# A hybrid decoder layer on one core: softmax statistics exchanged by ScalarE and GpSimd, opening weights ranked first on VectorE, last weight sums formed in the fourth product

## The chip, the cores and the metric

The kernel runs as one program on one NeuronCore of a Trainium2 chip. The metric is the device time of that core in microseconds (us); lower is better. The engines are named PE (TensorE, matrix products), PEld (its weight loads), DVE (VectorE), ACT (ScalarE), POOL (GpSimd) and SP (SyncE, which here only issues transfers).

## The reference

One layer over 1024 tokens of width 1024, float32 throughout:

```python
def reference(x, w_in, ..., w_out, ln1_w, ln1_b, mlp_w1, mlp_w2, ln2_w, ln2_b):
    h = hybrid_mixer(x, ...)     # z = x @ w_in (1024 -> 2816 columns), split into
                                 #  (A) state-space groups, (B) 4 retention heads,
                                 #  (C) 8 dilated-attention heads; y @ w_out
    x = layer_norm(ALPHA * x + h, ln1_w, ln1_b)
    h = square(relu(x @ mlp_w1)) @ mlp_w2      # 1024 -> 4096 -> 1024
    return layer_norm(ALPHA * x + h, ln2_w, ln2_b)

def dilated_attention_mixer(q, k, v):          # branches (128, 1), (512, 4), (2048, 16)
    outs, lses = branch results and their log-sum-exps
    return sum(softmax(lses)[..., i] * outs[i] for i in range(3))
```

## The kernel before, in words

**Precision.** Every large product is made of three float32r products: each operand is cast to float32r by ACT (the high part), the rest is subtracted by DVE or POOL (the low part), and `mm3` (from L402) issues high x high, high x low, low x high.

**Who sets the order.** The program is a set of coroutines with ranks. A planner with its own clock starts, at each step, the coroutine step that can begin earliest; where starts tie, the lower rank goes first. What comes out is a fixed order of instructions for every engine, executed in that order; semaphores only hold an instruction until its data are there. Tiles of 128x1024 ("units") come from one pool of 32, and a load has to wait for a free unit. Each kind of use leaves a number of units spare.

**Attention.** Heads go in pairs. `far` makes the scores of one head for the later half of the tokens in two layouts (`y` = 0 and 1), with row minima and exponential sums in a small tile `stat`. `join(p)` then has to bring the two layouts' statistics together: they live on other partitions of each other, so 16 blocks of 32 partitions are copied crosswise. From both statistics it works out one factor for each row, `fac`, by which `high` scales the far scores before it transposes them and multiplies them with the values. Meanwhile PE has the matmuls of the input projection (`dense`) and of the output projection to fill its time.

**First LayerNorm.** `out_a` finishes the output projection tile by tile; `add_a`, `norm1` and `x_operands` normalise each of the 8 token tiles on DVE, ACT and POOL, store it, transpose it on PE and split it into the operands of the first MLP product. Those for products 1 and 2 (tile `XOB`) need token tiles 0 to 3 only; products 6 and 5 (`XOA`), 7, 4 and 3 need all eight.

**The MLP products.** Both are done by a seven-product scheme on 2x2 blocks (products numbered 1 to 7, in the order `UORD = (1, 6, 5, 7, 2, 4, 3)` for the first). The first one runs over 16 quads of 256 hidden columns. Of the first `NF = 4` quads ("opening quads") products 1 and 2 are done early, in `mlp`, because they need only `XOB`: `up_load` brings half of such a quad's weights, `up_cast` casts them and `up_lo` makes the low parts (tile `wop`). Then come products 6, 5, 7, 4, 3 of each opening quad. Product 7 adds to the bank of product 6, product 4 adds to it again, and between them DVE must read the bank out (`up_evac`, tiles `u` and `rb`).

**The second MLP product** goes product by product (`DORD = (1, 5, 6, 3, 2, 7, 4)`), each over 8 parts `j` of the hidden width, 24 matmuls for each part. `down_load` brings for each part one tile of stored activations (`rraw`) and one or two of weights (`wraw`); `down_split` forms the weight sum where one is needed, in place in a resident tile `K`, and splits both into `doh` and `dol`. Loads run ahead by two parts, in the last two products by four.

**Second LayerNorm.** As soon as products 7 and 2 are in, tiles 0 to 3 are normalised under the last product; tiles 4 to 7 follow at the end. `layer_norm` multiplies by the weights on DVE and adds the bias on DVE below the column `LNB[t]` and else on POOL.

Of the kernel before, what the change touches and what calls it, by code (L numbers as in the profile page):

```python
# [16 lines left out]
ALU = mybir.AluOpType  # L17
# [10 lines left out]
NQ = FF // 256  # L28
NF = 4
# [7 lines left out]
LNF = "AAAADDD"  # L37
LNN = (1024,) * 5 + (512, 512)
LNW = (0,) * 6 + (512,)
LNB = (0,) * 7  # L40
TIE = 0.02
LAG = 2
DEPTH = 5
# [254 lines left out]
async def when(w, early=0.0):  # L298
    if isinstance(w, str):
        await ask(("flag", w))  # L300
    elif w:
        await ask(("data", w, early))
# [3 lines left out]
def trunk_kernel(ctx: ExitStack, tc: tile.TileContext, t_in, out):  # L306
    nc = tc.nc
    clock = Clock()
    pe, act, dve, pool, sp = (Engine(e, n, clock) for e, n in (
        (nc.tensor, "pe"), (nc.scalar, "act"), (nc.vector, "dve"), (nc.gpsimd, "pool"), (nc.sync, "sp")))  # L310
# [25 lines left out]
    st_ = Stream(clock)  # L336
# [13 lines left out]
    def free(*tiles):  # L350

        for t in tiles:
            if isinstance(t, (list, tuple)):
                free(*t)
            else:
                room = st_.room[tags.pop(t.tensor.name)]
                room[0] += 1
                room[1].append(clock.last[t.tensor.name])

    def U(shape, dt=F32, name="u", spare=2):  # L360
        return take(up, shape, dt, "u", NU, name, spare)
# [7 lines left out]
    def PM(shape=(128, 512), name="pm"):  # L369
        return take(pp, shape, F32, "main", 3, name, 0)  # L370

    def PS(shape=(128, 512), name="ps"):
        return take(pp, shape, F32, "side", 5, name, 0)

    def SM(shape, name, bufs=2):
        return take(sm, shape, F32, name, bufs, name, 0)

    def f(ap):
        return ap.bitcast(F32)

    async def tt(eng, o, a, b, op):
        await eng.tensor_tensor(out=o, in0=a, in1=b, op=op)
# [7 lines left out]
    M, A_, SUB = ALU.mult, ALU.add, ALU.subtract  # L390
# [796 lines left out]
    def counted(key, n):  # L1187
        count[key] = count.get(key, 0) + 1
        return count[key] == n
# [61 lines left out]
    async def far(i_, h):  # L1251
# [39 lines left out]
        if counted(("far", p), 2):  # L1291
            st_.add(1.7, join(p))

    async def join(p):

        stat = T["stat", p]
        for i in range(4):
            for j in range(4):
                a, b = slice(32 * i, 32 * i + 32), slice(32 * j, 32 * j + 32)
                await act.copy(stat[b, 2, i], stat[a, 1, j])  # L1300
                await dve.tensor_copy(stat[b, 3, i], stat[a, 0, j])
        await when([stat])
        both = stat.rearrange("p (o y) j e k -> p o (y j e) k", o=2)
        wk = await SM([128, 3, 16], "wk")
        tmp = await SM([128, 2, 16], "wk2")
        await tt(dve, wk[:, 0], both[:, 0, :, 0], both[:, 1, :, 0], ALU.min)
        await tt(dve, tmp, wk[:, 0:1].to_broadcast([128, 2, 16]), both[:, :, :, 0], SUB)
        await act.activation(tmp, tmp, AF.Exp)
        await tt(dve, wk[:, 1:3], tmp, both[:, :, :, 1], M)
        await tt(dve, wk[:, 1], wk[:, 1], wk[:, 2], A_)  # L1310
        await dve.reciprocal(wk[:, 2], wk[:, 1])
        fac = await SM([128, 2, 4, 2], "fac")
        await tt(dve, fac.rearrange("p y j e -> p (y j e)"), tmp[:, 0], wk[:, 2], M)
        free(wk, tmp, stat)
        T["fac", p] = fac
        flag(f"fac{p}")
# [192 lines left out]
    async def layer_norm(t, w, b_, last=None):  # L1509
# [14 lines left out]
        if t < 7 or not last:  # L1524
# [13 lines left out]
            for a in range(D // n):  # L1538
                c = slice(a * n, (a + 1) * n)
                await tt(pool if last and c.start < LNW[t] else dve, v[:, c], v[:, c], w[:, c], M)  # L1540
                await tt(dve if last and c.start < LNB[t] else pool, v[:, c], v[:, c], b_[:, c], A_)
                if last:
# [12 lines left out]
    def big(tag, shape, name, dt=F32R):  # L1555
        t = bigp.tile(shape, dt, tag=tag, name=name)
        clock.avail[t.tensor.name] = clock.last[bigs[tag].tensor.name]
        bigs[tag] = t
        return t

    x1 = []
    raws, hls, hs = {}, {}, {}
# [253 lines left out]
    UORD = (1, 6, 5, 7, 2, 4, 3)  # L1816
# [34 lines left out]
    async def up_cast():  # L1851
        for q in range(NF):
            await when(f"ulf{q}")
            for n in (1, 2):
                op = await U([128, 2, 512], F32R, "wop", spare=3)
                await act.copy(op[:, 0], raws["f", q][:, n - 1])
                st_.add(6.2, up_lo(q, n, op, raws["f", q][:, n - 1], ("uf", q), 2, lambda q=q: free(raws.pop(("f", q)))))
        for q in range(NQ):
            for n in UORD if q >= NF else [n for n in UORD if n not in (1, 2)]:
                await when(f"ul{q}" if n in (1, 2, 4) else f"us{q}")  # L1860
# [2 lines left out]
                src = {1: lambda: wa[:, 0], 2: lambda: wa[:, 1], 4: lambda: wb[:, 1], 5: lambda: s1[:, 0],  # L1863
                       6: lambda: s1[:, 1], 7: lambda: s3[:, 0], 3: lambda: s3[:, 1]}[n]()
                op = await U([128, 2, 512], F32R, "wop", spare=3)
# [4 lines left out]
    async def up_lo(q, n, op, src, key, total, last):  # L1870
        await when([op[:, 0]])
        await tt(dve, op[:, 1], src, f(op[:, 0]), SUB)
        wop[q, n] = op
        flag(f"uw{q}.{n}")
        if counted(key, total):
            last()

    async def product(q, n, ps, first):
        await when(f"xo{n}")
        await when(f"uw{q}.{n}")  # L1880
        op = wop.pop((q, n))
        for k in range(4):
            w = slice(k * 128, (k + 1) * 128)
            await mm3(ps, op[:, 0, w], op[:, 1, w], *XO[n][k], first and k == 0, k == 3, True)
        free(op)
        st_.add(1, up_evac(q, n))

    async def up_mm(q, part):
        for n in part:
            if n in (1, 6, 5):  # L1890
                su[q, "ps", n] = await (PM() if n == 1 else PS())
                await product(q, n, su[q, "ps", n], True)
            else:
                await when(f"ue{q}.{ {7: 6, 2: 1, 4: 7, 3: 7}[n] }")
                await product(q, n, su[q, "ps", {7: 6, 2: 1, 4: 6, 3: 5}[n]], False)
# [75 lines left out]
    async def down_load():  # L1971

        K["t"] = None
        for i, n in enumerate(DORD):
            for j in range(NJ):
                if i == 0:
                    await when(f"uq{NQ - 1}" if j > 0 else f"uq{NQ - 2}")
                    await when(f"rd{2 * j + 1}")
                ahead = i * NJ + j - (2 if i < 5 else NL)
                if ahead >= 0:  # L1980
                    await when(f"dn{ahead // NJ}.{ahead % NJ}")
                if i == 0 and j == 0:
                    await when("bfree")
                    K["t"] = big("B", [128, NJ, 2, 512], "K", F32)
                ri, rk = ROP[n]
                r = await U([128, 2, 512], name="rraw", spare=4)
                await sp.dma_start(out=r, in_=r_d[j][ri][:, rk])
                blk = {1: (0,), 5: (1,), 6: (3,), 3: (3,), 7: (3, 1), 2: (2,), 4: (2,)}[n]
                ws = []
                for b_ in blk:  # L1990
                    w = K["t"][:, j] if n == 1 else await U([128, 2, 512], name="wraw", spare=4)
                    await sp.dma_start(out=w, in_=w2_d[b_, j].rearrange("p (a c) -> p a c", a=2))
                    ws.append(w)
                raws["d", n, j] = r, ws
                flag(f"dl{n}.{j}")

    async def down_split():
        for n in DORD:
            for j in range(NJ):
                await when(f"dl{n}.{j}")  # L2000
                r, ws = raws.pop(("d", n, j))
                k = K["t"][:, j]
                src = ws[0]
                if n in (5, 6, 4):
                    await tt(dve, k, ws[0], k, SUB)
                    free(ws)
                    src, ws = k, []
                elif n == 7:
                    await tt(dve, ws[0], ws[0], ws[1], SUB)
                    free(ws.pop())  # L2010
                if n == 1:
                    ws = []
                out = []
                for v in (r, src):
                    hi = await U([128, 2, 512], F32R, "doh", spare=2)
                    await act.copy(hi, v)
                    lo = await U([128, 2, 512], F32R, "dol", spare=2)
                    await when([hi])
                    await tt(dve, lo, v, f(hi), SUB)
                    out += [hi, lo]  # L2020
                free(r, ws)
                dop[n, j] = out
                flag(f"ds{n}.{j}")
# [69 lines left out]
    async def mlp():  # L2093
# [4 lines left out]
        for q in range(NQ):  # L2098
            flag(f"uq{q}")
            if q == NQ - 1:  # L2100
                await up_mm(q, (1, 6, 2))
                flag("bfree")
            await up_mm(q, (6, 5, 7, 4, 3) if q < NF else UORD if q < NQ - 1 else (5, 7, 4, 3))
        for n in (7, 4, 3):
            free([list(v) for v in XO["u", n]])
        flag("xfree")
# [59 lines left out]
```

## Time and profile before

| | |
|---|---|
| median of 3 runs | 1197.47 us (1197.14 to 1200.64) |
| the profiled execution | 1201.07 us, its span 1199.3 us, so 1.8 us lie around the span |
| mean granted TensorE clock | 0.976 |
| PE, PEld busy | 1134.2 us, 960.8 us |
| DVE, ACT, POOL busy | 835.2 us, 534.1 us, 246.1 us |
| HBM | 127.42 MB read, 46.91 MB written, 145 GB/s over the span |

The span is the time from the first to the last instruction of one execution. An engine counts as busy while an instruction of its own runs, and also while an instruction that has been started is held up. Matmuls are pipelined and their ends are modelled, so PE's busy share is no share of its peak. The granted clock is the share of full speed that TensorE had in a stretch.

### The profile page before, as it was taken

To read this page: it belongs to the slowest core of one execution; us is meant where nothing else is said; L and a number is where in the kernel's file an instruction comes from. 1 tells how busy PE (TensorE), PEld (TensorE's weight loads), DVE (VectorE), ACT (ScalarE), POOL (GpSimd) and SP (SyncE) were. 2 spreads that over 40 slices of the span, in tenths; PEclk is the share of its full clock that TensorE was granted. 3 is DMA by queue.
4 is the path that set the end of the run, shared out by engine and by line. 5 is a ranking of instruction groups with operands and counts; after the bars stand their busy time and mean duration, and the time that the engine had idled before them with its cause. 6 is when DMAs were issued, how large, how long until landed. Compare 5 with 4: busy or idle time off the path is not lost.

```text
span 1199.3 us, 15952 instructions
## 1 busy us (share of the span) xinstructions
PE 1134.2 (95%) x5825; PEld 960.8 (80%) x5825; DVE 835.2 (70%) x1737; ACT 534.1 (45%) x941; POOL 246.1 (21%) x155
## 2 busy tenths in 40 slices
PE   8999998998999899996999999999999999999987
PEld 7889887878988688875777888888788888888765
DVE  5986486676743889888577666666556785376995
ACT  5122313674756657234444545445444443332430
POOL 1131317442155433455000000000000000000503
PEclk9999999997999999997999999999999999999988
DMA  8001423320160424033264344353489565667651
GB/s 311 18 1 32 141 63 99 140 106 1 36 227 36 177 105 150 31 119 123 80 208 169 130 169 155 139 181 123 171 319 368 180 207 181 206 217 257 216 188 71
DMA packets 65134, 175.37 MB, mean 146 GB/s; under 512 B 7064, under 2 KB 16800, under 8 KB 65056
## 3 DMA queue, kind: packets, MB, share of 16 engines
q1 hardware_dynamic: 65056, 174.35, 41.4%
q8 instruction: 46, 0.75, 0.3%
q14 instruction: 32, 0.26, 0.1%
HBM read 127.42 MB, written 46.91 MB: 145 GB/s over the span
## 4 chain that ended last, share of the span: by engine, by line
PE 70%; DVE 17%; issue 6%; ACT 3%; DMA 2%; POOL 2%; SPq 0%; DVEq 0%; POOLq 0%; ACTq 0%
PE pm L394 32%; PE ps L394 26%; PE ps_o L394 3%; DVE par L234 2%; PE ps_f L394 2%; DVE park L234 2%; DVE X L234 2%; PE ps_pt L400 1%; DVE dol L234 1%; DVE stat L234 1%; PE ps_x L400 1%; DMA wraw<-in_mlp_w_units 1%; DVE far L234 1%; PE ps_y L394 1%; DVE s L234 1%
## 5 line engine op out<-in xcount | busy, mean ns | idle before, releaser
L234 POOL TENSOR_TENSOR lnr<-lnr,nhalf 128x1 f32<-128x1 f32 x16 | 11.5, 723 | 586.7 <-DVE lnmv L234 545.9
L394 PE MATMUL ps<-xoh,wop 128*128 128x512 f32 x384 | 123.9, 390 | 5.5 <-DVE u L234 5.5
L394 PE MATMUL pm<-doh 128*128 128x512 f32 x256 | 100.5, 393 | 7.5 <-DVE X L234 7.5
L394 PE MATMUL pm<-dol,doh 128*128 128x512 f32 x256 | 100.3, 392 | 0.0
L394 PE MATMUL pm<-doh,dol 128*128 128x512 f32 x256 | 100.3, 392 | 0.0
L234 DVE TENSOR_TENSOR dol<-rraw,doh 128x1024 fp32r<-128x1024 f32 x56 | 70.4, 1257 | 42.6 <-ACT doh L234 30.6
L234 ACT CAST doh<-rraw 128x1024 fp32r<-128x1024 f32 x56 | 58.7, 1048 | 82.4 <-DMA rraw<-r_d 63.0
L394 PE MATMUL pm<-XOB,wop 128*128 128x512 f32 x384 | 94.2, 395 | 0.0
L394 PEld LDWEIGHTS ps<-xoh,wop 128*128 128x128 f32 x384 | 72.1, 188 | 22.4 <-issue 4.3
L394 PE MATMUL ps<-XOA,wop 128*128 128x512 f32 x384 | 89.8, 389 | 0.0
L394 PE MATMUL pm<-XA,whi 128*128 128x512 f32 x224 | 89.0, 397 | 0.0
L394 PE MATMUL pm<-XA,wlo 128*128 128x512 f32 x224 | 88.8, 396 | 0.0
L394 PE MATMUL pm<-XB,whi 128*128 128x512 f32 x224 | 88.5, 395 | 0.0
L234 ACT ACTIVATE rb<-rb 128x512 f32<-128x512 f32 x64 | 40.5, 633 | 105.5 <-DVE rb L234 104.5
L394 PEld LDWEIGHTS pm<-XOB,wop 128*128 128x128 f32 x384 | 72.7, 191 | 14.8
L394 PEld LDWEIGHTS ps<-XOA,wop 128*128 128x128 f32 x384 | 72.1, 188 | 15.0
L234 POOL TENSOR_TENSOR wlo<-wraw,whi 128x1024 fp32r<-128x1024 f32 x24 | 58.3, 2441 | 117.7 <-ACT whi L234 102.5
L394 PE MATMUL ps<-xol,wop 128*128 128x512 f32 x192 | 74.7, 389 | 0.0
L394 PE MATMUL ps<-doh 128*128 128x512 f32 x192 | 74.7, 389 | 0.0
L394 PE MATMUL ps<-dol,doh 128*128 128x512 f32 x192 | 74.7, 389 | 0.0
L394 PE MATMUL ps<-doh,dol 128*128 128x512 f32 x192 | 74.7, 389 | 0.0
L234 ACT CAST doh<-K 128x1024 fp32r<-128x1024 f32 x32 | 33.7, 1054 | 66.0 <-DVE K L234 60.4
(287 smaller groups left out, 2862.2 us busy)
## 6 DMA issues: line engine op xcount, KB each, us to landing
wraw<-in_mlp_w_units SPq DMA_DIRECT2D x92, 512.0 KB
rraw<-r_d SPq DMA_DIRECT2D x56, 512.0 KB
r_d<-rs SPq DMA_DIRECT2D x32, 512.0 KB
wraw<-in_w_in_units SPq DMA_DIRECT2D x20, 512.0 KB
v_d<-v SPq DMA_DIRECT2D x8, 512.0 KB
w<-v_d SPq DMA_DIRECT2D x8, 512.0 KB
abias<-in_c_bias SPq DMA_DIRECT2D x8, 512.0 KB
wraw<-in_w_out SPq DMA_DIRECT2D x8, 512.0 KB
```

The lines of the kernel that those rows point to most:

```text
L234: fn(*a, **kw)
L394: nc.tensor.matmul(ps, a, b, start=start, stop=stop, skip_group_check=open_)
L400: nc.tensor.transpose(ps, a, idn)
```

## The change

Five edits, in the order of the diff:

1. The bias of the second LayerNorm is added by DVE, no longer by POOL, for token tiles 0 to 3.
2. In `join`, ACT copies both layouts' statistics in one instruction for each of the 16 blocks, and DVE's 16 copies go. The copies keep the order of `y`, so the partner of layout `y` is slot `3 - y`. Of the small operations behind the copies, DVE keeps the minimum (now two halves) and the reciprocal; POOL gets three subtractions, three multiplications, one addition and the last multiplication.
3. The low parts of the opening quads' products 1 and 2 get rank -3 instead of 6.2.
4. In the opening quads, product 6 of the next quad (for the fourth quad: product 1 of the fifth) is issued between products 7 and 4.
5. In the second MLP product, `K = w2 - K`, the weight sum of product 4, is formed during product 3, the fourth in order; its weight tile is loaded there as a third tile for each part. Product 4 loads activations alone.

```diff
-LNB = (0,) * 7
+LNB = (1024,) * 4 + (0,) * 3
...
-                await act.copy(stat[b, 2, i], stat[a, 1, j])
-                await dve.tensor_copy(stat[b, 3, i], stat[a, 0, j])
+                await act.copy(stat[b, 2:4, i], stat[a, 0:2, j])
         await when([stat])
-        both = stat.rearrange("p (o y) j e k -> p o (y j e) k", o=2)
         wk = await SM([128, 3, 16], "wk")
         tmp = await SM([128, 2, 16], "wk2")
-        await tt(dve, wk[:, 0], both[:, 0, :, 0], both[:, 1, :, 0], ALU.min)
-        await tt(dve, tmp, wk[:, 0:1].to_broadcast([128, 2, 16]), both[:, :, :, 0], SUB)
+        part = lambda y, k: stat[:, y, :, :, k].rearrange("p j e -> p (j e)")
+        half = lambda v, y: v[:, 8 * y:8 * y + 8]
+        own = stat[:, 0:2].rearrange("p y j e k -> p (y j e) k")
+        for y in range(2):
+            await tt(dve, half(wk[:, 0], y), part(y, 0), part(3 - y, 0), ALU.min)
+        await tt(pool, tmp[:, 0], wk[:, 0], own[:, :, 0], SUB)
+        for y in range(2):
+            await tt(pool, half(tmp[:, 1], y), half(wk[:, 0], y), part(3 - y, 0), SUB)
         await act.activation(tmp, tmp, AF.Exp)
-        await tt(dve, wk[:, 1:3], tmp, both[:, :, :, 1], M)
-        await tt(dve, wk[:, 1], wk[:, 1], wk[:, 2], A_)
+        await tt(pool, wk[:, 1], tmp[:, 0], own[:, :, 1], M)
+        for y in range(2):
+            await tt(pool, half(wk[:, 2], y), half(tmp[:, 1], y), part(3 - y, 1), M)
+        await tt(pool, wk[:, 1], wk[:, 1], wk[:, 2], A_)
         await dve.reciprocal(wk[:, 2], wk[:, 1])
         fac = await SM([128, 2, 4, 2], "fac")
-        await tt(dve, fac.rearrange("p y j e -> p (y j e)"), tmp[:, 0], wk[:, 2], M)
+        await tt(pool, fac.rearrange("p y j e -> p (y j e)"), tmp[:, 0], wk[:, 2], M)
...
-                st_.add(6.2, up_lo(q, n, op, raws["f", q][:, n - 1], ("uf", q), 2, ...
+                st_.add(-3, up_lo(q, n, op, raws["f", q][:, n - 1], ("uf", q), 2, ...
...
-                blk = {1: (0,), 5: (1,), 6: (3,), 3: (3,), 7: (3, 1), 2: (2,), 4: (2,)}[n]
+                blk = {1: (0,), 5: (1,), 6: (3,), 3: (3, 2), 7: (3, 1), 2: (2,), 4: ()}[n]
...
-                src = ws[0]
-                if n in (5, 6, 4):
+                src = ws[0] if ws else k
+                if n == 3:
+                    await tt(dve, k, ws[1], k, SUB)
+                    free(ws.pop())
+                if n in (5, 6):
...
-            await up_mm(q, (6, 5, 7, 4, 3) if q < NF else UORD if q < NQ - 1 else (5, 7, 4, 3))
+            if q < NF:
+                await up_mm(q, (5, 7) if q else (6, 5, 7))
+                await up_mm(q + 1, (6,) if q + 1 < NF else (1,))
+                await up_mm(q, (4, 3))
+            else:
+                await up_mm(q, UORD[1:] if q == NF else UORD if q < NQ - 1 else (5, 7, 4, 3))
```

## Rows read from the trace of the kernel before

**Rows 1.** The page's first part: busy us, share of the span, instructions.
```profile
PE 1134.2 (95%) x5825; PEld 960.8 (80%) x5825; DVE 835.2 (70%) x1737; ACT 534.1 (45%) x941; POOL 246.1 (21%) x155
```
**Rows 2.** Windows: busy of PE, PEld, DVE, ACT, POOL; clock; DMA share; GB/s.
```profile
270.00:275.00 5.00, 2.36 (x11) 2.36 (x12) 4.67 (x9) 0.99 (x4) 1.89 (x2) 0.65 0.00 0
275.00:280.00 5.00, 5.00 (x32) 5.00 (x31) 1.10 (x6) 2.62 (x4) 0.16 (x1) 0.66 0.00 0
...
405.00:410.00 5.00, 5.00 (x17) 3.97 (x16) 4.03 (x15) 2.58 (x6) 0.37 (x1) 0.69 0.02 5
```
**Rows 3.** Windows again, of the two later stretches.
```profile
538.18:586.19 48.01, 37.34 (x173) 30.39 (x172) 37.63 (x71) 23.99 (x51) 17.94 (x12) 0.82 0.38 126
...
1145.00:1150.00 5.00, 5.00 (x15) 3.90 (x15) 5.00 (x8) 0.00 (x0) 0.00 (x0) 0.62 1.00 397
```
**Rows 4.** Tile `stat`: ns min/median/max; then by line: busy us, mean ns.
```profile
L234 DVE COPY stat<-stat x64: 147/161/2326, 259.2 to 457.7; 32x4 f32<-32x4 f32 x64
...
L234 DVE COPY stat<-stat 32x4 f32<-32x4 f32 x64 | 22.3, 349 | 5.2 <-ACT far L234 4.3
...
L234 POOL TENSOR_TENSOR sqt<-mixp 128x256 f32<-128x256 f32 x6 | 3.9, 643 | 34.9 <-DVE mixp L234 34.9
...
L234 POOL TENSOR_TENSOR par<-ident 32x16 f32<-32x16 f32 x1 | 0.2, 206 | 0.0
```
**Rows 5.** Timeline around the joins: start us, us, instruction, [idle before <- releaser].
```profile
264.09 7.91 DVE L234 COPY stat<-stat 32x4 f32<-32x4 f32 x9
...
264.17 2.40 POOL L234 TENSOR_TENSOR wlo<-wraw,whi 128x1024 fp32r<-128x1024 f32 x1 [3.04 <-ACT whi L234]
...
272.64 0.90 PE L394 MATMUL ps_o<-pt,v 128*128 128x256 f32 x3 [3.29 <-DVE pt L234]
...
403.81 0.50 PE L394 MATMUL pm<-whi 128*128 128x512 f32 x1 [4.30 <-DVE X L234]
```
**Rows 6.** Timeline between the first LayerNorm and the first MLP product.
```profile
531.97 1.15 ACT L234 CAST wop<-wraw 128x512 fp32r<-128x512 f32 x2 [3.28 <-DMA wraw<-in_mlp_w_units]
...
559.79 0.71 PE L394 MATMUL pm<-XOB,wop 128*128 128x512 f32 x2
...
570.19 16.16 PE L394 MATMUL pm<-XOB,wop 128*128 128x512 f32 x70
...
559.82 1.42 DVE L234 TENSOR_TENSOR wop<-wraw,wop 128x512 fp32r<-128x512 f32 x1
...
563.02 0.68 DVE L234 TENSOR_TENSOR wop<-wraw,wop 128x512 fp32r<-128x512 f32 x1
...
572.63 0.68 DVE L234 TENSOR_TENSOR ws<-wraw 128x512 f32<-128x512 f32 x1
```
**Rows 7.** Waits from 565 to 640 us (total us, times, longest), and DVE's timeline there.
```profile
PE ps L394 <- DVE u L234: 2.9, 3, 1.2
...
PEld ps L394 <- DVE u L234: 1.2, 1, 1.2
...
589.72 1.29 DVE L234 TENSOR_TENSOR wop<-ws,wop 128x512 fp32r<-128x512 f32 x2
...
621.31 2.49 DVE L234 TENSOR_TENSOR wop<-ws,wop 128x512 fp32r<-128x512 f32 x4
```
**Rows 8.** Waits of PE from 1080 us on; timeline of DVE and POOL there.
```profile
PE pm L394 <- DVE X L234: 7.5, 1, 7.5
...
1095.36 1.23 DVE L234 TENSOR_TENSOR wraw<-wraw 128x1024 f32<-128x1024 f32 x1 [5.47 <-DMA wraw<-in_mlp_w_units]
...
1115.05 3.42 DVE L234 TENSOR_TENSOR dol<-wraw,doh 128x1024 fp32r<-128x1024 f32 x1
...
1137.21 3.37 DVE L234 TENSOR_TENSOR dol<-rraw,doh 128x1024 fp32r<-128x1024 f32 x1
...
1141.64 1.21 DVE L234 TENSOR_TENSOR K<-wraw,K 128x1024 f32<-128x1024 f32 x1
...
1132.90 6.60 POOL L234 TENSOR_TENSOR X<-X,lnrow 128x1024 f32<-128x1024 f32 x2 [2.28 <-DVE X L234]
```

More of the change, by code (lines that the diff above doesn't have):

```diff
@@ L1856, in up_cast @@
                 await act.copy(op[:, 0], raws["f", q][:, n - 1])
-                st_.add(6.2, up_lo(q, n, op, raws["f", q][:, n - 1], ("uf", q), 2, lambda q=q: free(raws.pop(("f", q)))))
+                st_.add(-3, up_lo(q, n, op, raws["f", q][:, n - 1], ("uf", q), 2, lambda q=q: free(raws.pop(("f", q)))))
         for q in range(NQ):
```

## The prediction, made before the changed kernel ran

> **What bounds the kernel now.** I read the page's busy times first. PE is busy for 1134.2 of 1199.3 us and no other engine for more than 835.2 [rows 1], so the matmuls set the time, and a change can gain only where PE stands still or runs at the lower of its two clock levels (1.2 and 2.4 GHz). The page's 40 slices and then windows say where that is: in the stage of the joins, between the first LayerNorm and the first MLP product, a little in the opening quads, and at the step from product 7 to product 4. In each of these stretches I took the list of waits to see who ends PE's wait, and that engine's timeline to see why it was late. The releaser is nearly always DVE. Its lateness has two sources: its own queue is full, or one of its instructions is held up while POOL runs. The second is plain in the joins: nine small copies of 32x4 take 7.91 us while POOL is in instructions of 2.40 us [rows 5], though the median of the 64 copies is 161 ns [rows 4].
>
> **Part A, the join (four times).** Removed: 64 copies, 22.3 us of DVE. At the median they would take 64 x 0.161 = 10.3 us, so 12.0 us are hold-ups behind POOL [rows 4]. ACT's 16 copies a join stay as many and carry 8 instead of 4 elements a partition: nothing. What PE loses by it: 3.29 us in the first join, where DVE reaches the low part of the transposed probabilities late, and 4.30 us in the third, where DVE empties a bank late [rows 5]. Behind both PE runs on at a lower granted clock: 5.00 x 0.34 + 2.36 x 0.35 = 2.5 us and 5.00 x 0.31 = 1.6 us [rows 2]. Together 11.7 us, the upper bound. Added: eight operations of 128x16 or 128x8 on POOL in each join. The trace has no such one; between 0.21 us (32x16) and 0.64 us (128x256) [rows 4] I take 0.21, the nearer size, 1.7 us a join, and handovers DVE, POOL, ACT, POOL, DVE, POOL. POOL is entered three times, and each time an instruction of 2.40 us may be ahead of it in its queue [rows 5]: up to 7.2 us for a `fac`. Behind a late `fac` stand the scaling of the far scores on DVE and all that DVE has queued after it. In the first three pairs the projections' matmuls cover that; in the last pair hardly anything does. So the bounds are a gain of 11.7 and a loss of 7.2. I take a gain of 4: the mechanism is clear, but the planner deals out the whole attention stage anew, and DVE's other operations there can still be held up by POOL. A rule speaks against this part: Perfetto Trace Analysis in the Trainium skill, section Optimizing Scalar/DVE Operations, says that moving work between DVE and GpSimd might not help, since they share a port of the memory. By it part A would be 0 and the sum 19. The trace shows the contention, 12.0 us of it in these copies, but this edit moves the copies to ACT and only the small rest to POOL, so I don't follow it all the way.
>
> **Part B, rank -3.** The opening quads' products 1 and 2 are PE's filler while LayerNorm ends: 96 matmuls, of which 70 are still to do at 570.19 [rows 6]. From 538.18, the first of them, to 586.19, where the products that need all tokens begin, PE is busy for 37.34 of 48.01 us at a mean clock of 0.82 [rows 3]: idle 10.7, and clock 37.34 x 0.18 = 6.7, together 17.4 us, the upper bound. The filler is missing because its low parts come last on DVE: the casts of the second quad are done by 533.1, its first product starts at 559.79 and stops after two matmuls, for the low parts are made at 559.82 and 563.02 [rows 6]. With rank -3 they follow their casts, and PE has filler from about 540 on. The price: up to eight low parts at 0.68 us ahead of LayerNorm's chain, 5.4 us, if none of them ran ahead of its end anyway; that is the lower bound, a loss. What is late next: product 6 of the first quad needs its weight sums, which DVE makes from 572.63 on; four of them and a low part at 0.68 and a cast of 0.6 (half of the 1.15 for two) end at 572.6 + 5 x 0.68 + 0.6 = 576.6 [rows 6], and with handovers 577 to 578. If that stays where it is, the product starts at 578 and not at 586.2. Gain 8.
>
> **Part C, the opening quads.** Between products 7 and 4 of a quad PE waits for DVE to read out the bank: 2.9 + 1.2 us in four places [rows 7]. A product of 12 matmuls (12 x 0.23 = 2.8 us, from 16.16 us for 70 [rows 6]) now lies between, more than the longest wait of 1.2. Its weights have to be ready a product pair earlier. For the second quad they are (low parts at 589.7), for the fourth hardly: DVE makes them among four from 621.3 to 623.8 [rows 7], about where PE would want them. Of 4.1 I take 3; bounds 0 and 4.1. The bank and the unit that product 6 takes earlier cost nothing as long as the five side banks hold: two quads use four of them.
>
> **Part D, biases and product 4.** PE waits 7.5 us at the start of product 4 for DVE's evacuation of product 7 [rows 8] and then has a clock of 0.62 for 5.00 us, 1.9 us more [rows 3]: 9.4 together, the upper bound. DVE is late because four of its instructions of 128x1024 are held up behind the biases on POOL (the last two run there for 6.60 us on end); the first takes 3.42 and the last 3.37 us where one alone takes 1.21 [rows 8]. That is 4 x 2.2 = 8.8 us. Ahead of the evacuation DVE also forms three of product 4's eight sums, 3 x 1.21 = 3.6. Both go; the four biases come, 4 x 1.21 = 4.8. DVE gets there 7.6 us earlier, just what PE waited for. The eight sums and eight loads are now in product 3, where a part takes PE 24 x 0.23 = 5.5 us and DVE then has three operations of 1.21, 3.6 us: hidden by the matmuls. If that cover fails, they cost what they are late (a rival below). I take 8; the lower bound is 0, if product 4's activations are last then.
>
> **The sum.** 4 + 8 + 3 + 8 = 23 us. The profiled execution took 1201.07 us, so 1178.1 by its own time; the median of the runs shown is 3.6 us below it, so 1174.5 against them. PE's work as such, the end of the last LayerNorm and the number of transfers stay.
>
> **The rivals.**
>
> *DVE is the bound at LayerNorm.* DVE is busy for 37.63 of those 48.01 us [rows 3]; what goes first delays the rest, and PE's transposes come late by as much as the filler gains. Part B then costs some 2 us: 1197.5 - 15 + 2 = 1184.5. For it: the rest of DVE's queue is on the way to product 6. Against it: PE's filler is worth 16.16 us and is now spent after the chain has ended. Chance 0.16.
>
> *The join's chain on POOL comes late.* All three entries meet a long instruction and the last pair has no cover: part A is -7, the time 1197.5 - 19 + 7 = 1185.5. Against it: POOL is busy for only 21% of the span [rows 1]. Beside it stands the GPSIMD Engine Reference in the Trainium skill, section Engine selection, which gives two-input elementwise work to VectorE and not to GpSimd. Chance 0.10.
>
> *More comes back.* All four parts near their upper bounds (10, 12, 4 and 9): 1162.5. Chance 0.08.
>
> *The fourth product starves, and the kernel is slower.* A part of product 3 needs three tiles now. In product 7, which has three already, DVE waits 5.47 us for a weight tile [rows 8]. If each of product 3's eight parts waited so, that would be 43.8 us, less a lead of two parts (11): 32.8 more, 1174.5 + 33 = 1207. It decides from 4.3 us a part ((23 + 11) / 8). Against it: product 7's parts were asked for four parts ahead and PE never waited within it; a wait of DVE alone costs nothing. Chance 0.07.
>
> *Nothing comes of it.* The planner's new order puts other waits where these were: 1195 to 1200. Chance 0.05.
>
> **How the numbers follow.** The forecast has the remaining 0.54, its own range 1167 to 1183. 1174.5 is predicted. The range 1161 to 1190 takes in the three neighbouring rivals with the bounds of A and B, and leaves out about 0.12. A difference of 0.3% (3.6 us) is about what a measurement can tell from none here. Faster by more: 0.54 + 0.16 + 0.10 + 0.08 = 0.88; same 0.05; slower 0.07.
>
> **What would show it.** A: no copies of DVE in `stat`, no wait of PE over 2 us around the joins, and `fac` no later behind the last copy than before. B: PE's share from the first `XOB` product to the first `XOA` product near 100% and the clock near 1, that stretch some 8 us shorter. C: no waits of PE for `u`. D: at the start of product 4 a wait below 1 us, no two-input operation of DVE over 2 us there, and PE without gaps in product 3. I would be wrong if the joins' stage grew by more than a few us, if PE waited for DVE's normalisation at 550 to 575 as long as now, or if product 3 showed gaps.

## The result, and the profile after

The changed kernel takes 1170.8 us in the median of four runs (1166.88 to 1172.16), the kernel before 1197.97 us (1197.14 to 1200.64): a ratio of 0.9764, with a 95% interval from 0.9735 to 0.9793. Predicted were 1174.5 us with a range from 1161 to 1190. The profiled execution of the changed kernel took 1170.03 us, with a span of 1168.3. Of one experiment below (`d_stores_last`) three times are read and no trace, since its profiled execution ran at a mean granted clock of 0.65 from end to end and took 1593 us.

The whole was near the forecast, but its parts were not. I cut both spans at the first matmul on `XOB`, the first on `XOA` and the first of the second MLP product (for this last cut I take the end of the matmul before it, some 0.15 us after its own start); each stretch holds one part of the change, and PE has the same number of matmuls in it in every kernel below: 3061, 172, 1248 and 1344.

| Stretch, us | before | after | less | predicted |
|---|---|---|---|---|
| start to first `XOB` (A) | 538.2 | 526.6 | 11.5 | 4 |
| `XOB` to first `XOA` (B) | 48.0 | 31.9 | 16.1 | 8 |
| `XOA` to second MLP (C) | 289.9 | 289.8 | 0.2 | 3 |
| second MLP to the end (D) | 323.2 | 320.0 | 3.2 | 8 |

The page's first part, of the changed kernel (busy us, share, instructions):
```profile
PE 1122.4 (96%) x5825; PEld 950.5 (81%) x5825; DVE 814.3 (70%) x1665; ACT 532.3 (46%) x941; POOL 239.4 (20%) x183
```
PE's work is the same 5825 matmuls. It is busy 11.8 us less than in [rows 1], because fewer of them ran at the lower clock; the rest of the 31.0 us that the span lost is waiting.

**Stage A.** Windows of the changed kernel (busy of PE, PEld, DVE, ACT, POOL; granted clock; DMA share; GB/s), POOL's and PE's timeline around the first join, and one of PE's waits from 231 to 540 us; then one window of each kernel, before and after, from the first join to the first `XOB` product:
```profile
270.00:275.00 5.00, 5.00 (x44) 5.00 (x43) 3.36 (x4) 2.74 (x6) 4.89 (x7) 1.00 0.00 0
...
264.94 0.55 POOL L234 TENSOR_TENSOR wk<-wk,stat 128x16 f32<-128x16 f32 x3 [3.03 <-DVE wk L234]
265.73 2.40 POOL L234 TENSOR_TENSOR wlo<-wraw,whi 128x1024 fp32r<-128x1024 f32 x1 [0.25 <-ACT whi L234]
268.21 2.36 POOL L234 TENSOR_TENSOR Qs<-aq,Qs 64x1024 fp32r<-64x1024 f32 x1
270.64 2.89 POOL L234 TENSOR_TENSOR KL<-ak,KH 64x1024 fp32r<-64x1024 f32 x1
273.50 0.72 POOL L234 TENSOR_TENSOR wk<-wk,stat 128x16 f32<-128x16 f32 x3
...
275.33 0.24 POOL L234 TENSOR_TENSOR fac<-wk,wk 128x16 f32<-128x16 f32 x1 [0.36 <-DVE wk L234]
...
269.70 0.56 PE L394 MATMUL ps_o<-pt,v 128*128 128x256 f32 x3 [0.21 <-DVE pt L234]
...
PE pm L394 <- POOL MB L234: 3.4, 2, 2.3
```
```profile
263.60:538.18 274.58, 256.21 (x1464) 223.85 (x1462) 204.90 (x531) 153.93 (x368) 112.31 (x74) 0.96 0.28 98
...
263.84:526.64 262.80, 249.56 (x1464) 217.47 (x1462) 188.69 (x465) 154.54 (x366) 118.52 (x105) 0.99 0.29 103
```
Between 270 and 275 us PE had 2.36 us of work at a clock of 0.65 [rows 2]; now it is never idle there and keeps its clock. The wait of 3.29 us for `pt` [rows 5] is 0.21, with 1.02 for ACT's cast of `pt` just before it; the wait of 4.30 us for `X` isn't there any more. The join's second entry on POOL meets three long instructions in a row, 7.65 us of work from 265.73 to 273.50, just what the rival of the late chain feared. But `fac` is made at 275.33, 6 us earlier than the 281.4 of before, because its inputs come earlier, and PE has other work meanwhile. What is new is PE's 3.4 us of waits for `MB`, which stands in POOL's queue. Over the two long windows PE stands still for 13.2 us and not 18.4, and is busy for 249.6 us and not 256.2 with the same matmuls: more than half of the gain is clock.

**Stage B.** A window over the whole stretch, then PE's last filler and DVE's low parts and first sum of the changed kernel:
```profile
526.64:558.57 31.93, 30.96 (x173) 25.55 (x172) 28.92 (x59) 21.60 (x49) 19.16 (x12) 1.00 0.49 165
...
555.94 2.79 PE L394 MATMUL pm<-XOB,wop 128*128 128x512 f32 x11
558.57 0.61 PE L394 MATMUL ps<-XOA,wop 128*128 128x512 f32 x2
...
542.90 3.21 DVE L234 TENSOR_TENSOR wop<-wraw,wop 128x512 fp32r<-128x512 f32 x4
...
552.78 0.68 DVE L234 TENSOR_TENSOR ws<-wraw 128x512 f32<-128x512 f32 x1
```
In [rows 3] PE was busy for 37.34 of 48.01 us at a clock of 0.82; now it is for 30.96 of 31.93 at 1.00. When LayerNorm's last transposes are done, 11 matmuls of filler are left, where [rows 6] had 70. The first weight sum comes 26.1 us after the first `XOB` product and not 34.5.

**Stage C.** PE's waits from 556 to 860 us (total, times, longest), the longest of them, and the low parts that DVE makes up to its end:
```profile
PE ps L394 <- DVE wop L234: 3.6, 3, 2.2
PE ps L394 <- DVE u L234: 1.8, 1, 1.8
...
583.89 2.58 PE L394 MATMUL ps<-XOA,wop 128*128 128x512 f32 x10 [2.20 <-DVE wop L234]
...
578.94 0.69 DVE L234 TENSOR_TENSOR wop<-wraw,wop 128x512 fp32r<-128x512 f32 x1
...
581.95 0.68 DVE L234 TENSOR_TENSOR wop<-ws,wop 128x512 fp32r<-128x512 f32 x1
...
583.15 1.29 DVE L234 TENSOR_TENSOR wop<-ws,wop 128x512 fp32r<-128x512 f32 x2
```
The waits for `u` of [rows 7] have gone from the opening quads, but PE now waits for the weights of the product put in between: 2.20 us in the second quad and 0.97 in the third. DVE makes the low parts of the second quad's products 4 (578.94) and 3 (581.95) first, and only then that of the third quad's product 6 (583.15), for which PE waits. Two of the waits shown are not part C's: 0.4 us for `wop` come at the first product on `XOA`, and 1.8 us for `u` in the last of the 16 quads, where the kernel before waits for 1.55.

**Stage D.** SP's queue, ACT, DVE and PE where product 4 begins, and a window there, all of the changed kernel:
```profile
1103.20 0.34 SPq L234 DMA_DIRECT2D out<-X  x1
...
1103.64 0.37 SPq L234 DMA_DIRECT2D rraw<-r_d  x1
...
1106.61 0.34 SPq L234 DMA_DIRECT2D out<-X  x1
1107.04 2.76 SPq L234 DMA_DIRECT2D rraw<-r_d  x4
...
1107.63 1.05 ACT L234 CAST doh<-rraw 128x1024 fp32r<-128x1024 f32 x1 [4.96 <-DMA rraw<-r_d]
...
1108.71 1.22 DVE L234 TENSOR_TENSOR dol<-rraw,doh 128x1024 fp32r<-128x1024 f32 x1 [2.13 <-ACT doh L234]
...
1111.64 1.04 ACT L234 CAST doh<-rraw 128x1024 fp32r<-128x1024 f32 x1 [2.00 <-DMA rraw<-r_d]
...
1111.82 0.57 PE L394 MATMUL pm<-doh 128*128 128x512 f32 x1 [2.38 <-DVE X L234]
...
1115.19 0.79 PE L394 MATMUL pm<-doh 128*128 128x512 f32 x1 [0.67 <-DVE X L234]
...
1110.00:1130.00 20.00, 17.51 (x64) 13.69 (x65) 17.38 (x19) 9.68 (x10) 0.00 (x0) 0.83 0.32 115
```
The 7.5 us of [rows 8] have become 2.38 and 0.67, with a clock of 0.83 behind them. No instruction of DVE is held up any more. What is late now is a load: each store `out<-X` waits at the head of SP's queue until DVE has added the bias, and the activations' loads are issued only behind it. ACT's cast waits for the load, DVE's low part for the cast, and the evacuation of `X` stands behind that low part in DVE's queue (1110.99 us).

### The profile page after: what moved, and what is told of

It is laid out like the page before. It is cut to its first block, busy times and chain, and to the rows that moved or that the text cites. A ratio compares the mean times of both kernels' runs of the same rounds, so it can differ in the third digit from the quotient of the medians.

```text
span 1168.3 us, 15903 instructions
## 1 busy us (share of the span) xinstructions
PE 1122.4 (96%) x5825; PEld 950.5 (81%) x5825; DVE 814.3 (70%) x1665; ACT 532.3 (46%) x941; POOL 239.4 (20%) x183
## 4 chain that ended last, share of the span: by engine, by line
PE 44%; DVE 4%; DMA 1%; issue 1%; ACT 1%; SPq 0%; DVEq 0%; POOL 0%
PE ps L394 27%; PE pm L394 17%; DVE dol L234 1%; DVE X L234 1%; DMA wraw<-in_mlp_w_units 1%; DMA rraw<-r_d 0%; DVE rs L234 0%; DMA K<-in_mlp_w_units 0%; DVE wop L234 0%; DVE SQ L234 0%; DVE ws L234 0%; ACT rb L234 0%; ACT X L234 0%; ACT doh L234 0%; DVE rb L234 0%
## 5 line engine op out<-in xcount | busy, mean ns | idle before, releaser
L394 PEld LDWEIGHTS ps<-xoh,wop 128*128 128x128 f32 x384 | 72.1, 188 | 17.4 <-DVE u L234 2.2
L394 PEld LDWEIGHTS pm<-doh 128*128 128x128 f32 x256 | 48.6, 190 | 14.3 <-issue 2.8
```

The source lines that it names most:

```text
L394: nc.tensor.matmul(ps, a, b, start=start, stop=stop, skip_group_check=open_)
```

## Experiments

Their times stand beside runs of the kernel before on the same chip, whose median was 1198 to 1203 us, so times from different runs are compared by their ratios. "Before plus" starts from the kernel before and "after with" from the changed one. The stretches are read from every trace in the same way:

| Kernel | first `XOB` | to `XOA` | to second MLP | to the end | ratio to before (95%) |
|---|---|---|---|---|---|
| before | 538.2 | 48.0 | 289.9 | 323.2 | 1 |
| after | 526.6 | 31.9 | 289.8 | 320.0 | 0.9764 (0.9735 to 0.9793) |
| `a_join_only` | 528.6 | 47.0 | 291.9 | 323.3 | 0.9908 (0.9881 to 0.9934) |
| `a_smalls_on_dve` | 531.9 | 31.9 | 293.3 | 317.6 | 0.9816 (0.9789 to 0.9843) |
| `a_join_back` | 536.5 | 31.9 | 290.7 | 320.2 | 0.9831 (0.9783 to 0.9880) |
| `b_rank_only` | 534.1 | 31.9 | 290.9 | 324.1 | 0.9863 (0.9837 to 0.9890) |
| `c_order_only` | 538.7 | 47.9 | 289.6 | 323.3 | 0.9973 (0.9952 to 0.9994) |
| `c_order_back` | 525.5 | 31.9 | 291.3 | 317.8 | 0.9753 (0.9722 to 0.9783) |
| `c_cast_order` | 527.6 | 31.9 | 287.7 | 319.6 | 0.9706 (0.9662 to 0.9749) |
| `d_last_only` | 535.3 | 48.0 | 289.8 | 317.6 | 0.9956 (0.9932 to 0.9981) |
| `d_bias_on_pool` | 525.0 | 32.0 | 289.3 | 324.0 | 0.9778 (0.9748 to 0.9808) |
| `d_sum_in_last` | 529.7 | 31.9 | 291.5 | 319.4 | 0.9734 (0.9678 to 0.9790) |
| `d_stores_last` | | | | | 0.9713 (0.9685 to 0.9740) |
| `best` | 525.1 | 31.9 | 287.8 | 313.5 | 0.9666 (0.9648 to 0.9683) |

A stretch with the same state of its part repeats within 1 us in the second column, within some 5 us in the first and within 1 to 4 us in the last two.

### The join

**`a_join_only`**: before plus the change's `join`, nothing else.

> The kernel before with the new join alone (part A). Theory: the copies behind POOL were what held DVE up in the joins' stage, so this part alone takes the stage up to the first XOB product from 538.2 to about 527 us, and the whole time falls by 8 to 12 us (1186 to 1190 against 1198). Rival 1, the join gains only the 4 us of the prediction and the rest of the 11.5 us came from the planner's new order with the other parts: 1194 and a first XOB product at about 534. Rival 2, the port that DVE and POOL share makes it worth nothing: 1197 to 1199.

Measured 1190.62 us beside 1201.28 for the kernel before, first `XOB` product at 528.6. The stage's gain comes with the join alone; rival 1 and rival 2 fall.

**`a_smalls_on_dve`**: after with the join's eight small operations on DVE; ACT still makes all copies.
```
-        await tt(pool, tmp[:, 0], wk[:, 0], own[:, :, 0], SUB)
+        await tt(dve, tmp[:, 0], wk[:, 0], own[:, :, 0], SUB)
...
-        await tt(pool, fac.rearrange("p y j e -> p (y j e)"), tmp[:, 0], wk[:, 2], M)
+        await tt(dve, fac.rearrange("p y j e -> p (y j e)"), tmp[:, 0], wk[:, 2], M)
```


> The changed kernel with the join's small operations back on DVE (the swapped halves are still copied by ScalarE, so no copies on DVE). Theory: what part A gains is the copies' leaving DVE; the small operations on POOL matter little, so this is within 2 us of the changed kernel (1169 to 1173). Rival 1, half of the gain is the small operations' leaving DVE: 1176. Rival 2, the handovers to POOL cost something and this is faster: 1166 to 1168.

Measured 1177.34 us, where `c_order_back`, with the changed kernel's join, took 1169.32 on the same chip. My theory falls and rival 1 stands. The first `XOB` product is at 531.9, some 5 us later than with the operations on POOL. The operations `wk<-wk,stat` of this kernel (ns min/median/max), DVE in its first join, two windows; then the same operations on POOL in the changed kernel:
```profile
L234 DVE TENSOR_TENSOR wk<-wk,stat x24: 154/161/1926, 262.3 to 452.3; 128x8 f32<-128x8 f32 x16, 128x16 f32<-128x16 f32 x8
...
269.08 2.51 DVE L234 TENSOR_TENSOR wk<-wk,stat 128x16 f32<-128x16 f32 x3
...
261.30:531.90 270.60, 256.83 (x1464) 224.57 (x1462) 200.02 (x497) 155.99 (x366) 113.03 (x73) 0.96 0.28 100
...
470.00:480.00 10.00, 10.00 (x46) 9.51 (x46) 7.85 (x14) 3.96 (x7) 0.73 (x1) 0.50 0.13 41
```
```profile
L234 POOL TENSOR_TENSOR wk<-wk,stat x24: 196/203/397, 264.9 to 450.6; 128x8 f32<-128x8 f32 x16, 128x16 f32<-128x16 f32 x8
```
On DVE the small operations are held up as the copies were, up to 1.93 us for one of 0.16. On POOL each takes 0.04 us more at the median, and none over 0.40. PE waits for `s` for 6.4 us where the changed kernel has 3.2, but not for `MB`: from the first join on it stands still for 13.8 us in all, the changed kernel for 13.2. The loss is nearly all clock, most of it behind the fourth join: PE stops five times between 458 and 468 us, for 3.2 us in sum, and then runs at 0.50, the lower level, from 470 to 480. That the held-up small operations make these stops is not shown.

**`a_join_back`**: after with the old `join`.

> The changed kernel with the old join (parts B, C and D stay). Theory: part A is worth in company about what it is worth alone (0.9908, 11 us), half by the copies and half by the small operations that leave DVE: 1181 to 1184, the first XOB product some 10 us later. Rival: part of A's 11 us and of B's 16.4 us are the same microseconds, since the sum of the four parts alone is 36 us and the whole 28: 1174 to 1178.

Measured 1180.53 us, just below the theory's range, and 0.0067 of before, 8 us, more than the changed kernel by the ratios, which lies between the theory and the rival's 3 to 7 us. The stretches decide: the first `XOB` product comes 9.9 us later, and PE waits again for `pt` (3.3 us at the longest) and for `X` (4.3). That part A and part B share microseconds isn't seen in them: A's is as long in company as alone, and so is B's.

### The rank

**`b_rank_only`**: before plus one number.
```
-                st_.add(6.2, up_lo(q, n, op, raws["f", q]
+                st_.add(-3, up_lo(q, n, op, raws["f", q]
```


> The kernel before with rank -3 for the opening quads' low parts alone (part B). Theory: early low parts alone fill PE while LayerNorm ends; the stretch from the first XOB to the first XOA product falls from 48.0 to about 32 us, the whole time by 14 to 17 us (1181 to 1184). Rival 1, half of the 16.1 us that this stretch lost came from a DVE that part A had relieved: the stretch is about 40 us, the time 1190. Rival 2, DVE is the bound at LayerNorm and its chain comes as late as before: 1196, product 6 of the first quad begins no earlier after the last attention matmul.

Measured 1183.60 us with a stretch of 31.9 us: the theory stands, both rivals fall. A window over the stretch, PE's end of the filler and DVE's low parts and first sum in this kernel:
```profile
534.14:566.00 31.86, 30.95 (x174) 25.56 (x173) 28.83 (x59) 21.64 (x49) 19.18 (x12) 1.00 0.48 165
...
563.00 0.60 PE L400 MATMUL ps_x<-ident,t 128*128 128x128 f32 x4
563.35 2.77 PE L394 MATMUL pm<-XOB,wop 128*128 128x512 f32 x11
...
550.33 3.19 DVE L234 TENSOR_TENSOR wop<-wraw,wop 128x512 fp32r<-128x512 f32 x4
...
560.18 0.68 DVE L234 TENSOR_TENSOR ws<-wraw 128x512 f32<-128x512 f32 x1
```
It is the changed kernel's stretch to within 0.1 us. Counted from the first `XOB` product, the last transposes come at 28.9 us and not 31.7, and 11 matmuls follow them and not 70: 2.8 us by the chain and 13.4 us by the filler, together 16.2.

### The opening quads

**`c_order_only`**: before plus the change's order of products in `mlp`.

> The kernel before with the new order of the opening quads' products alone (part C). Theory: the waits for u (4.1 us) go and waits for low parts (wop) of about the same sum take their place, because the next quad's product 6 is asked for earlier than DVE makes its weights: 1197 to 1199, no difference, XOA to the second MLP's first product 290 us as before. Rival: the part gains its 3 us by itself (1195) and lost them only beside part B, whose rank changed the order of DVE's work in the opening quads.

Measured 1197.93 us, a ratio of 0.9973 whose interval ends just below 1; the stretch is 289.6 us against 289.9. PE waits 3.2 us for `wop` there, in the second and third quads, and 2.4 for `u`, all in the last of the 16 quads. The ratio alone, 3.2 us, would fit the rival; the stretch and the waits say that they were exchanged, and that the rank isn't to blame.

**`c_order_back`**: after with the old order.

> The changed kernel with the old order of the opening quads' products. Theory: the new order gains nothing, since its 5.4 us of waits (3.6 for low parts, 1.8 for u) stand in place of the 4.1 us for u: 1169 to 1173, and the waits for wop in the stretch after the first XOA product go while those for u come back. Rival: the new order still gains its 3 us and something else in that stretch loses them: 1174.

Measured 1169.32 us, no different from the changed kernel, and `u` is waited for again, in each opening quad (4.5 us) and in the last one:
```profile
PE ps L394 <- DVE u L234: 6.1, 5, 1.6
PE ps L394 <- DVE wop L234: 0.4, 1, 0.4
```

**`c_cast_order`**: after with ACT's casts in PE's order.
```
+        for q in range(NF):
+            todo += [(q, n) for n in ((5, 7) if q else (6, 5, 7))]
+            todo += [(q + 1, 6 if q + 1 < NF else 1), (q, 4), (q, 3)]
+        for q in range(NF, NQ):
+            todo += [(q, n) for n in (UORD[1:] if q == NF else UORD)]
-        for q in range(NQ):
-            for n in UORD if q >= NF else [n for n in UORD if n not in (1, 2)]:
+            for q, n in todo:
```


> The changed kernel, with ScalarE's casts of the opening quads' weights in the order in which PE now takes them (the next quad's product 6 before products 4 and 3 of this one; before, it came after them). Theory: the new order of products lost its 3 us because its weights are still cast in the old order; with this the waits for wop (3.6 us) and u (1.8 us) between the first XOA product and the second MLP fall below 1 us, and the time is 4 us less, 1167. Rival: these waits were in nobody's way or others take their place (the three buffers of the weights, DVE's sums): 1170 to 1172.

Measured 1165.01 us. PE's waits over the same stretch:
```profile
PE ps L394 <- DVE u L234: 2.0, 1, 2.0
PE ps L394 <- DVE wop L234: 0.4, 1, 0.4
```
The two late weights are gone (0.4 us is left at the first product on `XOA`), and the stretch is 287.7 us, as in `best` with 287.8, 2.1 less than after, 3.1 less than the mean of the five traces with the old order (290.8). So the order gives its predicted 3 us, which is about what PE waited for the two weights (3.2), once the casts follow it. The wait for `u` of 2.0 us, in the last quad, was not touched: there my expectation (both below 1 us) missed.

### The last product

**`d_last_only`**: before plus `LNB` and the sums in product 3.

> The kernel before with the biases on DVE and product 4's sums in product 3 (part D). Theory: it gains about 3 us (1195), since a wait of PE of some 3 us remains at the start of product 4: the loads for its activations stand behind stores of finished tiles on SP's queue. Rival: alone it gains the predicted 8 us (1190), and the 3.2 us of the whole change come from how the other parts moved the loads' times.

Measured 1195.32 us, ratio 0.9956, 5.3 us (2.3 to 8.2), and 5.6 us by the last stretch: halfway between theory and rival. PE waits 3.5 us at the start of product 4, as the theory has it.

**`d_bias_on_pool`**: after with `LNB = (0,) * 7`.

> The changed kernel with the last LayerNorm's biases back on POOL, product 4's sums still in product 3. Theory: the hold-ups of DVE behind POOL come back, two to four operations of 128x1024 take over 3 us, and product 4 starts some 3 to 5 us later: 1174 to 1176. Rival: the loads on SP's queue set product 4's start in any case, and the biases cost nothing: 1170 to 1172.

Measured 1173.38 us, by its ratio not to be told from the changed kernel, and 4.0 us more in the last stretch. PE's wait at product 4, DVE's and POOL's timelines and SP's queue in this kernel:
```profile
PE pm L394 <- DVE X L234: 7.5, 1, 7.5
...
1102.91 3.44 DVE L234 TENSOR_TENSOR dol<-rraw,doh 128x1024 fp32r<-128x1024 f32 x1
1106.27 3.39 DVE L234 TENSOR_TENSOR dol<-K,doh 128x1024 fp32r<-128x1024 f32 x1
...
1101.94 6.64 POOL L234 TENSOR_TENSOR X<-X,lnrow 128x1024 f32<-128x1024 f32 x2 [1.99 <-DVE X L234]
...
1105.29 3.65 SPq L234 DMA_DIRECT2D out<-X  x2
1109.05 1.67 SPq L234 DMA_DIRECT2D rraw<-r_d  x3
```
The hold-ups are back, and PE waits the very 7.5 us of [rows 8], though the three sums are out of DVE's way here.

**`d_sum_in_last`**: after with the sums in product 4 again.
```
-                blk = {1: (0,), 5: (1,), 6: (3,), 3: (3, 2), 7: (3, 1), 2: (2,), 4: ()}[n]
+                blk = {1: (0,), 5: (1,), 6: (3,), 3: (3,), 7: (3, 1), 2: (2,), 4: (2,)}[n]
```


> The changed kernel with the last weight sums back in product 4 (the biases stay on DVE). Theory: the sums are 3.6 us of DVE ahead of the evacuation of product 7, so that PE waits some 3 us longer at the start of product 4 and falls to its lower clock for longer: 1174 to 1176. Rival: the loads on SP's queue set that start, and the sums cost nothing there: 1170 to 1172; then they may even be the better place.

Measured 1170.44 us, no different from the changed kernel by its ratio, with a last stretch of 319.4 us against 320.0, and a wait of 2.8 us against 3.0. My theory falls. The sums' place is worth nothing here; what part D gains comes from the biases.

**`d_stores_last`**: after with the first four tiles' stores behind all loads.
```
-            return sp.dma_start(out=out_d[t * 128:(t + 1) * 128, c], in_=x1[t][:, c])
+            if t < 4:
+                await when(f"dl4.{NJ - 1}")
+            await sp.dma_start(out=out_d[t * 128:(t + 1) * 128, c], in_=x1[t][:, c])
```


> The changed kernel, with the stores of output tiles 0 to 3 issued only after all loads of the last products (the same stores, later on the queue). Theory: the 3.05 us of waits at the start of product 4 come from loads queued behind these stores on SP; without them PE starts product 4 with under 1 us of wait and keeps its clock, 3 to 5 us less: 1166 to 1168. Rival 1, DVE's own order (an evacuation behind another tile's multiplications) sets the start: no change, 1170 to 1172. Rival 2, the stores pile up at the end and the end comes later: 1172 to 1176.

Measured 1165.10, 1165.18 and 1166.58 us, ratio 0.9713: the theory's size. The trace that shows the mechanism is the next kernel's.

### Both mends

**`best`**: after with the edits of `c_cast_order` and `d_stores_last`.

> The changed kernel with both mends: the casts of the opening quads in PE's order, and the stores of output tiles 0 to 3 issued after all loads of the last products. Theory: the two stand in different stages (559 to 620 and 1110 to 1120) and add up: the waits for wop and the waits for X at the start of product 4 are each below 1 us, and the time is 0.96 to 0.968 of before (1154 to 1163 where before takes 1202). Rival: the earlier start of the loads is taken back by DVE's order, PE still waits 2 to 3 us for X at product 4, and only the casts' gain is left: 0.970 to 0.973.

Measured 1159.57 us (1157.88 to 1160.92), ratio 0.9666. SP's queue and the window of stage D in this kernel:
```profile
1100.26 11.20 SPq L234 DMA_DIRECT2D rraw<-r_d  x4
1111.51 44.50 SPq L234 DMA_DIRECT2D out<-X  x12
...
1110.00:1130.00 20.00, 20.00 (x90) 16.53 (x90) 11.72 (x16) 5.62 (x6) 1.06 (x2) 1.00 0.35 132
```
The loads go out before the stores, PE waits for no `X` at all between 1050 and 1150 us, and its clock stays at 1.00. The last stretch takes 313.5 us, 5.3 less than the mean of the six traces with all of part D. The edit is the same as in `d_stores_last`, so this is what that kernel's theory said. This version is faster than both kernels.

## Why the prediction was right in sum and wrong in its terms

From the table, with means over the traces that share a part's state (old join 5, new join 7; old rank 4, new rank 9; old order 5, new order with old casts 6; old biases and sums 4, all of part D 6): A 536.6 - 526.9 = 9.7, B 47.7 - 31.9 = 15.8, C 290.8 - 290.7 = 0.1, D 323.5 - 318.8 = 4.7, in sum 30.3 us. Predicted were 23. Every part lies within its bounds; A and B came out above the value that I took, C and D below.

**Part A, 9.7 for 4.** The mechanism was right as far as it went: the two waits that I had priced, for `pt` and for `X`, go with the old join and come back with it. Mis-sized was the term of the small operations, which I moved to POOL at a cost of 1.7 us a join and no gain. Up to the 1601st matmul (261 to 266 us) PE's order is the same in all kernels; from there to the first `XOB` product the five traces with the old join take 271.0 to 275.0 us (mean 273.5), the seven with the new one 261.7 to 264.0 (263.0), and `a_smalls_on_dve` takes 270.6. So part A is worth 10.5 us by this count, and 7.6 of them need the small operations off DVE (one trace), though the priced waits are gone in that kernel too. Its loss is clock, which I had reckoned only behind the waits that I saw.

I took a gain of 4 because `fac` might come late. It is made earlier in every join, but the sign that I named is mixed: behind the last copy it comes after 10.7, 3.2, 3.2 and 3.1 us in the four joins, before after 9.4, 2.0, 7.4 and 4.8. Of the other two signs, DVE has no copies in `stat` any more, and PE does wait for over 2 us once: 2.3 for POOL's `MB`.

The Perfetto Trace Analysis in the Trainium skill (section Optimizing Scalar/DVE Operations) warns that work moved between DVE and GpSimd might not help. It helped here in both directions: these operations went from DVE to POOL, and the biases of part D from POOL to DVE. The GPSIMD Engine Reference in the Trainium skill (section Engine selection) puts GpSimd at about twice VectorE's time for two-input elementwise work. For the small operations it is less here, medians of 203 and 161 ns.

**Part B, 15.8 for 8.** PE's share and clock came out as named. The step that failed is "if that stays where it is": I held the weight sums at 572.6 and let product 6 of the first quad wait for them. Counted from the first `XOB` product they came 8.3 us earlier too, since the low parts that stood ahead of them in DVE's queue [rows 6] were done long before and LayerNorm's chain ended 2.8 us earlier. With that, nearly the whole upper bound of 17.4 came back. The sums are still next in line: PE's first product on `XOA` waits 0.41 us for its low part. The rival of a DVE that is the bound at LayerNorm falls by `b_rank_only`: DVE is busy for 28.83 of 31.86 us there, but the chain's last transposes come earlier and not later.

**Part C, 0.1 for 3.** The four waits for `u` between products 7 and 4 went, as predicted. What failed is the readiness of the weights: I had found the second quad's in time, the fourth quad's "about where PE would want them", and didn't look at the third's. The casts on ACT, which make the order of DVE's low parts, were not in my account at all: the third quad's product 6 met a late weight by 2.20 us and the fourth's by 0.97. `c_cast_order` shows that this was what was missing.

**Part D, 4.7 for 8.** The hold-ups behind the biases were rightly named: with the biases on DVE no two-input operation of DVE takes over 1.23 us there, and with them back on POOL the wait of 7.5 us comes back whole. Two terms failed. The sums, 3.6 us of DVE's work, were worth nothing. And when DVE was no longer late, the loads behind the stores on SP's queue were: 3.05 us of waits and the lower clock behind them, against under 1 us named. The edit of `d_stores_last` gives 5.3 us more, and 4.7 + 5.3 = 10.0 is about the upper bound of 9.4. I had named product 4's activations only as the case in which nothing is gained, and did not look at what stands before their loads on SP, though the store waits there for the bias that I moved. Product 3 had no gaps of PE, so the rival of the starving product falls.

The rival "more comes back" came true in A and B and not in C and D. That the sum was near is luck in part: +5.7 and +7.8 against -2.9 and -3.3.

What stays open: by ratios the four parts alone make 11.0 + 16.4 + 3.2 + 5.3 = 36 us and the whole 28 (interval 25 to 32). The four share one set of runs of before, and each has an interval of some 3 us to either side, so I don't read an interaction from it; the stretches show none.

## What to carry to other kernels

Where an engine's short instructions are held up behind another's long ones, count every short one that is left or moved, not only those held up in the trace today: one of 0.16 us took up to 1.93. And read PE's clock as well as its waits: in `a_smalls_on_dve` PE waits about as long as in the changed kernel and loses its time at the lower level. When an operation is brought forward, follow the whole chain of those who prepare it, the cast ahead of the low part ahead of the product, and give all of them the same order. And when a compute step is moved, look at the queue in which a store waits for it: a store that is early in a queue makes every load behind it late.

## What the runs showed of the hardware

Two executions with the same order of instructions on every engine need not agree to better than 3 us up to the first MLP product. `d_last_only` has the order of before up to 984 us, yet its last far scores start at 450.1 us and those of before at 453.1. The granted clock tells them apart already from 200 to 300 us, in the window of before and that of `d_last_only`:
```profile
200.00:300.00 100.00, 88.81 (x503) 77.88 (x501) 69.59 (x157) 64.70 (x134) 43.12 (x21) 0.90 0.28 97
```
```profile
200.00:300.00 100.00, 88.70 (x517) 77.83 (x516) 72.00 (x158) 67.10 (x136) 42.64 (x21) 0.93 0.27 97
```
PE is equally busy in both, but spends more of the time at the lower of its two levels in one of them. The five kernels after, `c_cast_order`, `d_bias_on_pool`, `d_sum_in_last` and `best`, with one order up to there, reach the first `XOB` product at 525.0 to 529.7 us. So the 11.5 us of stage A in the first table are good to some 3 us, and the means over traces are the better figures.
